# Second attention: the query and key weight chunks are multiplied by the norm's weights on POOL in place of VectorE

## The chip, the cores and the metric

The kernel runs on one core of a Trainium2 chip. The core has five engines that run side by side, each through its own list of instructions in order: TensorE (PE in the profile, its weight loads PEld), VectorE (DVE), ScalarE (ACT), GpSimd (POOL) and SyncE (SP), which here only issues DMAs. Semaphores make one engine wait for another. The metric is the device time of one execution in microseconds (us).

## The reference

The reference is an encoder trunk of two layers over 512 frames of 1024 features in float32. The first layer is latent attention with 8 heads and a SwiGLU feed-forward part of 2816 hidden features. A shared key and value is then projected from the result, and the second layer attends to it with 16 heads of 64 features and a learned bias by relative position, followed by another SwiGLU part. Every part stands between two RMS norms. What concerns the change is the input of the second attention:

```
def rms_norm(x, g):
    y = x * lax.rsqrt(jnp.mean(x * x, axis=-1, keepdims=True) + EPS)
    return y * g

h  = rms_norm(x, attn_pre_g[1]);  q  = h @ w_q
kv = rms_norm(x, g_src) @ w_kv          # keys and values
```

The norm's weight g belongs to an input feature, so it can be multiplied into the rows of w_q and w_kv in place of x.

## The kernel before

Activations lie transposed, features on the 128 partitions and the 512 frames along a row. A float32 product is made from three float32r matmuls: each operand is split into a rounded part hi (ScalarE, a cast, line 144, or a scaled copy, line 148) and the rest lo = raw - hi (VectorE, line 145 or 149), and hi·hi, lo·hi and hi·lo are added up in PSUM (mm3, lines 356 to 358). So every weight goes once through ScalarE and once through VectorE.

The class Feed brings the weights. Its plan is a list of chunks of 128x1024, in the order of use. load issues a chunk's DMA on SP into one of 5 buffers "raw", two chunks ahead of split, and split writes whi and wlo, one chunk ahead of use. A chunk of the shared values (in_w_v) has two norm weights per partition, which enter as the scale of lines 148 and 149. A chunk of queries or keys (in_w_qkb) has eight, one for every 128 columns; the list gain holds them as a broadcast 128x8x128, and VectorE multiplies the raw chunk by it in place (line 306) ahead of the split. There are 16 such chunks, two (query, key) for each of eight pairs of heads. The plan has four value chunks, the first two of these, four value chunks, and then the other fourteen.

Around the first of these chunks the feed-forward part of layer 1 ends. Its last step is the class After: the sums of squares ss go through line 1288 and 1289 (VectorE) into ssv, POOL takes the power -0.5 (line 1292, tile r), ScalarE scales the result y by it (line 1298), TensorE transposes y (line 1319, tile yt), and VectorE adds it to the residual x (line 1322), which is split into xh and xl. This is done for each half of the frames; between the transposes stand the matmuls of the values on the half that is ready. Then the squares of x are summed (acc, line 426), POOL takes the power for the norm of the second attention (line 452, r), VectorE copies it to rtk (line 1493), TensorE spreads it (line 469, bc) and ScalarE scales the values by it. In the attention TensorE is kept busy by a generator (fill_b) that makes the queries and keys of the next pair of heads between the scores of this one; POOL writes a masked corner into each head's bias tile (line 1502).

The order of instructions on each engine is set by a scheduler when the kernel is built, from the order of the code, priorities (first) and its own estimates of time.

Of the kernel before, what the change touches and what calls it, by code (L numbers as in the profile page):

```python
# [14 lines left out]
OP = mybir.AluOpType  # L15
# [53 lines left out]
def trunk(ctx: ExitStack, tc: tile.TileContext, a, out):  # L69
    nc = tc.nc  # L70
    V = nc.vector
# [10 lines left out]
    def name_(n):  # L82
        uid[0] += 1
        return f"{n}_{uid[0]}"

    def U(dt=F32, name="u"):
        return up.tile([P, S], dt, tag="u", name=name_(name), bufs=NU)
# [4 lines left out]
    def bank(tag="mm", name="b"):  # L92
        return ps.tile([P, S], F32, tag=tag, name=name_(name), bufs={"mm": 4, "s": 2, "t": 2}[tag])
# [49 lines left out]
    def split(dst_hi, dst_lo, src):  # L143
        return (nc.scalar.copy(dst_hi, src),  # L144
                V.tensor_tensor(dst_lo, src, dst_hi.bitcast(F32), op=OP.subtract))  # L145

    def split_scaled(dst_hi, dst_lo, src, col):
        return (nc.scalar.activation(dst_hi, src, AF.Copy, scale=col),  # L148
                V.scalar_tensor_tensor(dst_lo, src, col, dst_hi.bitcast(F32), op0=OP.mult, op1=OP.subtract))  # L149

    class Pair:
# [13 lines left out]
        def load(self, j):  # L165

            if j == 0:
                self.raw[4], self.raw[5] = self.tile(2), self.tile(3)
            elif j in (1, 2):
                self.raw[j] = self.tile(j - 1)  # L170
# [81 lines left out]
    class Feed:  # L252
# [20 lines left out]
        def load(self, i):  # L273
            while len(self.raw) <= min(i, len(self.plan) - 1):
                src, n, j, _ = self.plan[len(self.raw)]
                if isinstance(src, Down):
                    src.load(*j)
                    self.raw.append(None)
                    continue
                if isinstance(src, Pair):  # L280
                    src.load(j)
                    self.raw.append(None)
                    continue
                t = wp.tile([P, 1024], F32, tag="raw", name=name_("raw"), bufs=5)
                if self.gate is not None:
                    nc.gpsimd.tensor_copy(t[:1, :1], self.gate[:1, :1])
                nc.sync.dma_start(t[:, :n], src[:, :n])
                self.raw.append(t)

        def split(self, i):  # L290
            while len(self.ready) <= min(i, len(self.plan) - 1):
                j = len(self.ready)
                self.load(j + 2)
                raw, (src, n, gain, room) = self.raw[j], self.plan[j]
                for f in range(j, min(j + 8, len(self.plan))):
                    if f < j + 5 and isinstance(self.plan[f][0], Pair) or isinstance(self.plan[f][0], Down):
                        self.load(f)
                if isinstance(src, Down):
                    src.sums(*gain)
                    raw = src.at[gain]  # L300
                elif isinstance(src, Pair):
                    src.sums(gain)
                    raw = src.raw[gain]
                elif gain is not None and gain.shape[1] > 2:
                    rv = raw[:, :n].rearrange("p (a b) -> p a b", a=gain.shape[1])
                    V.tensor_tensor(rv, rv, gain, op=OP.mult)
                    gain = None
                if room is None:
                    at_ = 24 if isinstance(src, Pair) else 0
                    pieces = [tuple(wp.tile([P, 1152], F32R, tag=t, name=name_("w" + t), bufs=3)[:, at_:at_ + 1024]  # L310
                                    for t in ("hi", "lo"))]
                else:
                    pieces = self.room[room]()
                w = pieces[0][0].shape[1]
                if isinstance(raw, list):
                    c = 0
                    for t in raw:
                        c_ = slice(c, c + t.shape[1])
                        split(pieces[0][0][:, c_], pieces[0][1][:, c_], t)
                        c += t.shape[1]  # L320
                for c in range(0, 0 if isinstance(raw, list) else n, w):
                    m = min(w, n - c)
                    with ExitStack() as st:
                        for b in self.behind.get(j, ()):
                            st.enter_context(tc.issue_after(b.ins))
                        if gain is None or isinstance(src, Pair):
                            split(pieces[c // w][0][:, :m], pieces[c // w][1][:, :m], raw[:, c:c + m])
                            continue
                        for d in range(0, m, S):
                            split_scaled(pieces[c // w][0][:, d:d + S], pieces[c // w][1][:, d:d + S],  # L330
                                         raw[:, c + d:c + d + S], gain[:, (c + d) // S, 0:1])

                def at(c, m, pieces=pieces, w=w):
                    o = c % w
                    return tuple(t[:, o:o + m] for t in pieces[c // w])

                self.ready.append(at)
# [142 lines left out]
    class Head:  # L480
# [19 lines left out]
        def turn(self, qt):  # L500
            if self.pt is None:
                self.pt = [pool[0].tile([P, NQT, S], F32R, tag=t, name=name_(t), bufs=n)
                           for t, n in (("pth", 2), ("ptl", 1))]
            n = P * (qt + 1)
            p = self.p.pop(qt)
            t = bank("t", "pt")
            for kt in range(qt + 1):
                nc.tensor.transpose(t[:, kt * P:(kt + 1) * P], p[:, kt * P:(kt + 1) * P], ident)  # L508
            tv = t[:, :n].rearrange("p (a b) -> p a b", b=P)
            q_ = slice(qt * P, (qt + 1) * P)  # L510
            split(self.pt[0][:, :qt + 1, q_], self.pt[1][:, :qt + 1, q_], tv)
# [155 lines left out]
    class Split:  # L667
# [5 lines left out]
        def each(self, k, h):  # L673
            c = HALF[h]
            if len(self.xs) <= k:
                self.xs.append((U(F32R, "xh"), U(F32R, "xl")))
            t = cut(self.xs[k], c)
            if self.gain is None:
                split(*t, self.x[k][:, c])
            else:  # L680
                split_scaled(*t, self.x[k][:, c], g(self.gain, k))
# [111 lines left out]
    for j in range(2):  # L793
        t = U(name="ckv")
# [49 lines left out]
    for j in range(2):  # L844
        V.tensor_tensor(ckv[j], ckv[j], rkv, op=OP.mult)
        h, l = U(F32R, "ckh"), U(F32R, "ckl")
        feed.behind[13] = feed.behind[14] = split(h, l, ckv[j])
        cks.append((h, l))
# [740 lines left out]
    b = [bank(), bank(), bank("s"), bank("s")]  # L1589
# [101 lines left out]
```

## Time and profile before

| | |
|---|---|
| median of 3 runs | 1132.62 us (1131.86 to 1137.13) |
| profiled execution | 1131.57 us, of which the span is 1129.8 us |
| TensorE busy | 1108.2 us (98%) |
| VectorE busy | 931.9 us (82%) |
| ScalarE busy | 686.0 us (61%) |
| POOL busy | 74.9 us (7%) |
| chain that ended last | TensorE 86%, VectorE 6%, ScalarE 3% |

The span is the time from the first to the last instruction in the profiler's record; the execution's own time is a little longer. A busy share is the time in which an engine ran an instruction; matmuls overlap, so a busy TensorE need not be at its peak. The chain is followed back from the last instruction, at each step to what released it. Around the change the span reads like this: to 535 us the feed-forward part of layer 1 ends, from 527 to 590 the values and the first query and key are made, from 597 to about 740 runs the second attention.

### The profile page before, as it was taken

What the parts mean: (1) busy time and instruction counts of PE and PEld (TensorE: products, weight loads), DVE (VectorE), ACT (ScalarE), POOL (GpSimd) and SP (SyncE); (2) the same over time, 40 slices, a digit from 0 to 9 for tenths busy, and PEclk for the clock granted to TensorE, in tenths of its full rate; (3) what the DMA queues carried; (4) which work ended last, traced back from release to release, by engine and by line L of the source; (5) the groups of instructions that cost most, each with busy time, mean ns of one, the idle gap of its engine ahead of it and who ended that gap; (6) DMA issues with size and microseconds to landing.
All of it is one profiled execution on the core that took longest, in us unless ns stands there. A gap on an engine that the chain in (4) does not pass through costs nothing.

```text
span 1129.8 us, 18992 instructions
## 1 busy us (share of the span) xinstructions
PE 1108.2 (98%) x6973; PEld 984.7 (87%) x6973; DVE 931.9 (82%) x1671; ACT 686.0 (61%) x1339; POOL 74.9 (7%) x106
## 2 busy tenths in 40 slices
PE   8999999999999999999999999999999999999997
PEld 6888889899999998887788888779899999998885
DVE  7787738999899889978757977647999999889977
ACT  6476637755555566668536777546755555566685
POOL 2200000100000002401000000000100000002402
PEclk9999999999999999999999999999999999999999
DMA  7433125323322449852356656625323322449923
GB/s 235 111 109 94 57 85 196 131 87 100 109 98 94 140 149 262 140 195 61 144 149 168 154 155 158 166 88 186 131 82 106 104 102 94 139 169 281 173 59 75
DMA packets 62990, 150.85 MB, mean 134 GB/s; under 512 B 8432, under 2 KB 10224, under 8 KB 62896
## 3 DMA queue, kind: packets, MB, share of 16 engines
q1 hardware_dynamic: 55552, 136.61, 38.3%
q0 software_dynamic: 6912, 12.59, 6.8%
q8 instruction: 55, 0.90, 0.3%
q10 hardware_dynamic: 432, 0.44, 0.1%
q14 instruction: 39, 0.32, 0.1%
HBM read 119.52 MB, written 9.63 MB: 114 GB/s over the span
## 4 chain that ended last, share of the span: by engine, by line
PE 86%; DVE 6%; ACT 3%; issue 2%; DMA 1%; POOL 1%; POOLq 0%; SPq 0%; DVEq 0%; ACTq 0%
PE al L1425 17%; PE b L356 10%; PE b L357 10%; PE b L358 10%; PE be L1425 9%; PE al L1185 8%; PE ga L1425 4%; PE be L1185 4%; PE de L1185 3%; PE ga L1185 3%; PE pt L508 2%; DVE wlo L145 1%; ACT whi L144 1%; PE b L1549 1%; PE b L1550 1%
## 5 line engine op out<-in xcount | busy, mean ns | idle before, releaser
L144 ACT CAST whi<-raw 128x1024 fp32r<-128x1024 f32 (+3 forms) x224 | 225.5, 1008 | 220.5 <-PE al L1425 73.3
L145 DVE TENSOR_TENSOR wlo<-raw,whi 128x1024 fp32r<-128x1024 f32 (+3 forms) x224 | 261.1, 1167 | 62.0 <-ACT whi L144 60.3
L1425 PE MATMUL al<-th,whi 128*128 128x256 f32 x432 | 123.0, 285 | 0.1
L1425 PE MATMUL al<-th,wlo 128*128 128x256 f32 x432 | 121.3, 281 | 0.0
L1425 PE MATMUL al<-tl,whi 128*128 128x256 f32 x432 | 121.1, 280 | 0.0
L356 PE MATMUL b<-xh,whi 128*128 128x512 f32 (+1 forms) x304 | 116.4, 383 | 1.8 <-ACT xh L148 1.8
L357 PE MATMUL b<-xl,whi 128*128 128x512 f32 (+1 forms) x304 | 112.8, 371 | 0.3 <-DVE xl L149 0.3
L358 PE MATMUL b<-xh,wlo 128*128 128x512 f32 (+1 forms) x304 | 112.7, 371 | 0.0
L174 DVE TENSOR_TENSOR raw<-raw,raw 128x1024 f32<-128x1024 f32 x72 | 86.7, 1220 | 0.6 <-DMA raw<-in_w_pair 0.3
L1425 PEld LDWEIGHTS al<-th,whi 128*128 128x128 f32 x432 | 81.3, 188 | 2.4 <-DVE ut L1437 0.3
L1425 PEld LDWEIGHTS al<-th,wlo 128*128 128x128 f32 x432 | 81.3, 188 | 0.3 <-DVE wlo L145 0.3
L1425 PEld LDWEIGHTS al<-tl,whi 128*128 128x128 f32 x432 | 81.4, 188 | 0.0
L496 ACT ACTIVATE p<-p,mn 128x128 f32<-128x128 f32 (+1 forms) x96 | 54.0, 562 | 31.8 <-DVE mn L494 31.6
L145 DVE TENSOR_TENSOR ptl<-pt,pth 128x128 fp32r<-128x128 f32 (+1 forms) x96 | 46.2, 486 | 28.8 <-ACT pth L144 23.0
L144 ACT CAST whi<-wd 128x512 fp32r<-128x512 f32 x86 | 49.9, 619 | 26.8 <-PE al L1185 11.9
L145 DVE TENSOR_TENSOR wlo<-wd,whi 128x512 fp32r<-128x512 f32 x86 | 56.5, 687 | 11.5 <-ACT whi L144 11.2
L356 PEld LDWEIGHTS b<-xh,whi 128*128 128x128 f32 x304 | 57.5, 189 | 9.6 <-ACT xh L148 2.7
L358 PEld LDWEIGHTS b<-xh,wlo 128*128 128x128 f32 x304 | 57.4, 189 | 8.9
L357 PEld LDWEIGHTS b<-xl,whi 128*128 128x128 f32 x304 | 57.5, 189 | 7.3 <-DVE xl L149 0.6
L144 ACT CAST pth<-pt 128x128 fp32r<-128x128 f32 (+1 forms) x96 | 40.3, 424 | 28.4 <-PE pt L508 27.8
L1185 PE MATMUL al<-whi,ph 128*128 128x512 f32 x132 | 51.9, 393 | 0.5 <-ACT y L1238 0.5
L1185 PE MATMUL al<-whi,pl 128*128 128x512 f32 x132 | 51.5, 390 | 0.0
(308 smaller groups left out, 3274.0 us busy)
## 6 DMA issues: line engine op xcount, KB each, us to landing
raw<-in_w_pair SPq DMA_DIRECT2D x72, 512.0 KB, 3.5
wd<-in_w_down SPq DMA_DIRECT2D x54, 256.0 KB, 5.9
raw<-in_w_o SPq DMA_DIRECT2D x16, 512.0 KB, 3.6
raw<-in_w_gu SPq DMA_DIRECT2D x16, 512.0 KB, 3.7
raw<-in_w_down SPq DMA_DIRECT2D x16, 512.0 KB, 4.4
raw<-in_w_qkb SPq DMA_DIRECT2D x16, 512.0 KB, 3.6
wd<-in_w_down POOLq DMA_DIRECT2D x22, 256.0 KB, 5.5
wd<-raw POOLq DMA_DIRECT2D x22, 256.0 KB, 4.2
```

The lines of the kernel that those rows point to most:

```text
L144: return (nc.scalar.copy(dst_hi, src), V.tensor_tensor(dst_lo, src, dst_hi.bitcast(F32), op=OP.subtract))
L145: V.tensor_tensor(dst_lo, src, dst_hi.bitcast(F32), op=OP.subtract))
L174: V.tensor_tensor(t, x, y, op=OP.add)
L356: nc.tensor.matmul(o, l[0], r[0], start=start, stop=False)
L357: nc.tensor.matmul(o, l[0], r[1], start=False, stop=False)
L358: nc.tensor.matmul(o, l[1], r[0], start=False, stop=stop)
L496: nc.scalar.activation(p[:, :n], p[:, :n], AF.Exp, bias=mn[:, :1], scale=-1.0, accum_out=self.sums[:, qt:qt + 1])
L508: nc.tensor.transpose(t[:, kt * P:(kt + 1) * P], p[:, kt * P:(kt + 1) * P], ident)
L1185: nc.tensor.matmul(to[e], l[c], r[d], start=j < 4 and k == 0 and n == 0, stop=k == NF // 2 - 1 and n == 2, skip_group_check=True)
L1425: nc.tensor.matmul(o, l[c], r[d], start=first_ and n == 0, stop=k == K2 - 1 and n == 2, skip_group_check=True)
L1549: nc.tensor.matmul(o[:, q_], vv, pth[:, kt, q_], start=kt == 0, stop=False)
L1550: nc.tensor.matmul(o[:, q_], vv, ptl[:, kt, q_], start=False, stop=kt == NQT - 1)
```

## The change

The multiplication by the norm's weights moves from split, where VectorE does it, to load, where POOL does it as soon as the chunk's DMA has landed. It is the same product, in place, on the same chunks; the value chunks are left as they were.

```diff
         def load(self, i):
             while len(self.raw) <= min(i, len(self.plan) - 1):
                 src, n, j, _ = self.plan[len(self.raw)]
+                gain = j
                 if isinstance(src, Down):
...
                 nc.sync.dma_start(t[:, :n], src[:, :n])
+                if gain is not None and gain.shape[1] > 2:
+                    rv = t[:, :n].rearrange("p (a b) -> p a b", a=gain.shape[1])
+                    nc.gpsimd.tensor_tensor(rv, rv, gain, op=OP.mult)
                 self.raw.append(t)
...
                 elif gain is not None and gain.shape[1] > 2:
-                    rv = raw[:, :n].rearrange("p (a b) -> p a b", a=gain.shape[1])
-                    V.tensor_tensor(rv, rv, gain, op=OP.mult)
                     gain = None
```

The scheduler places the new instructions. On POOL, from the last DMA of the feed-forward part on, this stood before (r is the power of line 1292 or 452, bias a head's bias tile):

```order
L250 DMA wd_5334<-raw_4942 128x512
L1292 TENSOR_TENSOR r_5979<-ssv_5099,mhalf 128x2
L1502 MEMSET bias_6440 64x64
L1502 MEMSET bias_6687 64x64
L1502 MEMSET bias_6832 64x64
L1292 TENSOR_TENSOR r_6187<-ssv_5099,mhalf 128x2
L452 TENSOR_TENSOR r_6436<-v_6434,mhalf 128x4
L1502 MEMSET bias_6938 64x64
```

In the changed kernel, whose lines after the edit have numbers that are 2 higher and where line 291 is the multiplication, it is this:

```order
L250 DMA wd_5334<-raw_4942 128x512
L291 TENSOR_TENSOR raw_6225<-raw_6225,gains 128x1024
L1294 TENSOR_TENSOR r_5979<-ssv_5099,mhalf 128x2
L1504 MEMSET bias_6441 64x64
L1504 MEMSET bias_6689 64x64
L1504 MEMSET bias_6834 64x64
L291 TENSOR_TENSOR raw_6245<-raw_6245,gains 128x1024
L1294 TENSOR_TENSOR r_6187<-ssv_5099,mhalf 128x2
L291 TENSOR_TENSOR raw_6584<-raw_6584,gains 128x1024
L454 TENSOR_TENSOR r_6437<-v_6435,mhalf 128x4
L291 TENSOR_TENSOR raw_6617<-raw_6617,gains 128x1024
```

Each of the three powers now has one multiplication directly ahead of it. The other thirteen multiplications follow, eight of them ahead of the fourth bias memset and the rest between the memsets.

On VectorE, around ssv of the second half (line 1289), this stood before:

```order
L149 SCALAR_TENSOR_TENSOR wv_6246<-raw_6205,gains,wv_6246 128x512 x2
L1289 SCALAR_TENSOR_TENSOR ssv_5099<-ss_0_5097,ssv_5099 128x2
L145 TENSOR_TENSOR wlo_6311<-raw_6225,whi_6310 128x1024
L426 TENSOR_TENSOR acc_6326<-acc_6326,sq_6328 128x256
L306 TENSOR_TENSOR raw_6244<-raw_6244,gains 128x1024
L426 TENSOR_TENSOR acc_6326<-acc_6326,sq_6331 128x256
L426 TENSOR_TENSOR acc_6326<-acc_6326,sq_6334 128x256
```

And now:

```order
L149 SCALAR_TENSOR_TENSOR wv_6248<-raw_6205,gains,wv_6248 128x512 x2
L1291 SCALAR_TENSOR_TENSOR ssv_5099<-ss_0_5097,ssv_5099 128x2
L145 TENSOR_TENSOR wlo_6312<-raw_6225,whi_6311 128x1024
L428 TENSOR_TENSOR acc_6327<-acc_6327,sq_6329 128x256
L428 TENSOR_TENSOR acc_6327<-acc_6327,sq_6332 128x256
L428 TENSOR_TENSOR acc_6327<-acc_6327,sq_6335 128x256
```

The multiplication is gone from between the additions, and the rest is as it was. SP's order of the chunks' DMAs stays the same here. In the attention itself, from the scores of the first heads on, the order of TensorE, VectorE and ScalarE differs in many places by a few instructions, since the scheduler weaves the queries and keys of the next heads into a changed timing.

## Rows read from the trace of the kernel before

**Rows 1.** The page's first part: busy time and share of each engine
```profile
PE 1108.2 (98%) x6973; PEld 984.7 (87%) x6973; DVE 931.9 (82%) x1671; ACT 686.0 (61%) x1339; POOL 74.9 (7%) x106
```

**Rows 2.** Windows: PE, PEld, DVE, ACT, POOL busy, clock, DMA, GB/s; last line 306 alone
```profile
720.00:740.00 20.00, 18.85 (x97) 14.19 (x96) 14.24 (x37) 13.06 (x34) 0.00 (x0) 1.00 0.52 131
...
600.00:660.00 60.00, 59.77 (x331) 50.08 (x330) 52.00 (x122) 43.96 (x111) 0.87 (x6) 1.00 0.65 169
...
600.00:660.00 60.00, 7.28 (x6) 1.00 0.65 169
```

**Rows 3.** TensorE's waits, 530 to 660 us: in total, times, longest
```profile
PE yt L1319 <- ACT y L1298: 2.9, 1, 2.9
```

**Rows 4.** The chain that ended last, 533 to 541 us: start, us, what
```profile
537.36 1.34 ACT y L1298 x2
...
538.74 0.69 PE yt L1319 x2
```

**Rows 5.** POOL's timeline: start, us, line, operation, idle before and releaser
```profile
512.40 0.83 POOL L1292 TENSOR_TENSOR r<-ssv,mhalf 128x2 f32<-128x2 f32 x1 [34.92 <-DVE ssv L1289]
...
533.98 3.35 POOL L1292 TENSOR_TENSOR r<-ssv,mhalf 128x2 f32<-128x2 f32 x1 [20.48 <-DVE ssv L1289]
557.55 1.01 POOL L452 TENSOR_TENSOR r<-v,mhalf 128x4 f32<-128x4 f32 x1 [20.23 <-DVE v L448]
...
777.96 0.70 POOL L452 TENSOR_TENSOR r<-v,mhalf 128x2 f32<-128x2 f32 x1 [59.74 <-DVE v L448]
792.02 2.21 POOL L452 TENSOR_TENSOR r<-v,mhalf 128x2 f32<-128x2 f32 x1 [13.37 <-DVE v L448]
```

**Rows 6.** VectorE's timeline around the power at 533.98
```profile
532.35 1.41 DVE L149 SCALAR_TENSOR_TENSOR wv<-raw,gains,wv 128x512 fp32r<-128x512 f32 x2
533.67 0.16 DVE L1289 SCALAR_TENSOR_TENSOR ssv<-ss,ssv 128x2 f32<-128x2 f32 x1
533.75 1.22 DVE L145 TENSOR_TENSOR wlo<-raw,whi 128x1024 fp32r<-128x1024 f32 x1
534.88 0.42 DVE L426 TENSOR_TENSOR acc<-acc,sq 128x256 f32<-128x256 f32 x1
535.22 1.22 DVE L306 TENSOR_TENSOR raw<-raw,gains 128x1024 f32<-128x1024 f32 x1
536.35 0.42 DVE L426 TENSOR_TENSOR acc<-acc,sq 128x256 f32<-128x256 f32 x1
540.25 0.43 DVE L426 TENSOR_TENSOR acc<-acc,sq 128x256 f32<-128x256 f32 x1 [3.48 <-ACT sq L425]
```

**Rows 7.** VectorE's timeline around the power at 792.02
```profile
792.12 1.22 DVE L174 TENSOR_TENSOR raw<-raw,raw 128x1024 f32<-128x1024 f32 x1
793.26 0.42 DVE L426 TENSOR_TENSOR acc<-acc,sq 128x256 f32<-128x256 f32 x1
```

**Rows 8.** The window behind TensorE's wait, columns as in rows 2
```profile
538.50:541.50 3.00, 2.76 (x8) 2.17 (x9) 0.43 (x1) 2.95 (x8) 0.00 (x0) 0.50 0.15 60
```

**Rows 9.** Line 306 (ns min/median/max); POOL's nearest multiplication (busy us, mean ns)
```profile
L306 DVE TENSOR_TENSOR raw<-raw,gains x16: 1173/1222/1226, 500.6 to 657.1; 128x1024 f32<-128x1024 f32 x16
...
L969 POOL TENSOR_TENSOR kr<-kr,sik 64x512 f32<-64x512 f32 x1 | 1.3, 1292 | 0.1
```

**Rows 10.** The second chunk's DMA issue on SP, and its time to landing
```profile
529.11 0.33 SPq L287 DMA_DIRECT2D raw<-in_w_qkb x1
...
DMA to landing us min/median/max: 3.4/3.4/3.4
```

**Rows 11.** VectorE around the power at 557.55, and TensorE's use of rtk
```profile
555.38 1.23 DVE L306 TENSOR_TENSOR raw<-raw,gains 128x1024 f32<-128x1024 f32 x1 [1.13 <-DMA raw<-in_w_qkb]
...
559.04 0.16 DVE L1493 COPY rtk<-r 128x4 f32<-128x4 f32 x1
...
560.98 0.49 PE L469 MATMUL bc<-ident,rtk 128*128 128x128 f32 x3
```

**Rows 12.** ScalarE's timeline: the cast of the third chunk
```profile
578.69 1.05 ACT L144 CAST whi<-raw 128x1024 fp32r<-128x1024 f32 x1 [4.10 <-issue]
```

## Prediction

> **What bounds the kernel now.** I read the page's first part, the windows over the second attention, TensorE's waits there, the chain at the one long wait, and last VectorE and POOL row by row around it. TensorE is busy for 1108.2 of 1129.8 us, VectorE for 931.9, POOL for 74.9 [rows 1]. In the stretch from 600 to 660 us, where six of the sixteen multiplications run, TensorE is busy for 59.77 of 60 us and VectorE for 52.00, of which the multiplications are 7.28 [rows 2]. So VectorE is heavily loaded there, but TensorE hardly ever waits for it.
>
> TensorE has one long wait between 530 and 660 us: 2.9 us before the transposes of line 1319 [rows 3]. The chain shows what stands behind it: POOL's power r of line 1292 runs from 533.98 to 537.33 [rows 5], ScalarE scales y by it (line 1298), and TensorE transposes y at 538.74 [rows 4]. This power is a 128x2 instruction. The same form takes 0.70 us at 777.96 and 2.21 at 792.02 [rows 5]; here it takes 3.35. What differs is VectorE: in the two slow cases it runs instructions on two SBUF operands back to back. At 533.75 these are a split, an addition, the multiplication of line 306 and an addition, to 536.77, and the power ends 0.56 us later [rows 6]; at 792.12 they are a sum and an addition, to 793.69, and it ends 0.54 us later [rows 7]. VectorE's own instructions keep their length (1.22 us). I read this as POOL being held off while VectorE works through such a run.
>
> The wait also costs clock. In the 3 us behind it TensorE is granted 0.50 of its clock (the 1.2 GHz level) [rows 8], where the stretches above have 1.00 (2.4 GHz) [rows 2]. Its 2.76 us of work there, eight matmuls, would take half as long at the full level: about 1.4 us lost.
>
> **The change, part by part.** VectorE loses sixteen multiplications of 1.22 us [rows 9], 19.5 us. POOL gets them. The trace has no POOL multiplication of 128x1024; the nearest is 64x512 at 1.29 us [rows 9], and twice the elements per partition make 2.58 us, my estimate, so 41 us in all on POOL, which was busy for 0.87 us between 600 and 660 [rows 2]. The bounds are 1.2 us (VectorE's own time, if POOL's cost were mostly fixed) and 5.2 us (twice as long, since POOL's 128x2 power is stretched three- to fivefold beside a busy VectorE). I take 2.58, the row of the same kind of instruction.
>
> *Relief of VectorE in the attention.* From 600 to 660 us TensorE has 0.23 us of idle time in all [rows 2], so the 7.28 us taken off VectorE can return no more than that there. The changed order also weaves some of TensorE's heads differently. I take 0 us. The ends are -0.5 (this idle time and as much around it) and +1.2 (a badly woven stretch: from 720 to 740 us TensorE is busy for 18.85 of 20 [rows 2]).
>
> *The thirteen multiplications behind the three powers.* Their lead is read from the third chunk: it is multiplied at 555.38, when it lands [rows 11], and its cast on ScalarE comes only at 578.69 [rows 12]. A POOL instruction of 2.58 or 5.2 us is hidden in these 23 us. The memsets of the bias tiles now stand between multiplications on POOL; each serves a head that begins later, and a delay of one multiplication is hidden too. 0 us.
>
> *The first chunk.* It stands ahead of the first power r of line 1292, at 512.40. VectorE's own multiplication of it begins at 500.6 [rows 9], so the chunk has landed by then; even 5.2 us of POOL end by 505.8, 6.6 us before that power [rows 5]. If VectorE is held for 2.58 us there and saved only 1.22, it is 1.4 us late. I take 0, with ends 0 and +1.4.
>
> *The second chunk: the term that counts.* The order puts its multiplication on POOL directly ahead of the power that this chain waits for. Queued behind it are that power, then ScalarE's scaling, the transposes, and TensorE with all that follows. The chunk is issued at 529.11 and lands 3.4 us later, at 532.5 [rows 10], 1.5 us before the power was begun. VectorE is in the wv splits then, which go over into ssv and the run [rows 6]. Without line 306 the run ends earlier: from 535.22 to 536.35 is 1.13 us, so it ends at 536.77 - 1.13 = 535.64. If POOL gets through only when the run ends, the multiplication goes from 535.64 to 538.22 and the power, 0.70 us alone, ends at 538.92 in place of 537.33: +1.6 us. If the multiplication gets in ahead of the wv splits and holds VectorE, ssv itself comes some 2.5 us late, the split and the additions follow, and the power ends at about 538.9 as well. The lower end is a multiplication that runs beside VectorE from its landing, 532.5 to 535.1; the power then waits only for the shorter run, 535.64 + 0.56 = 536.2, which is -1.1. The upper end is a multiplication of 5.2 us after the run: 535.64 + 5.2 + 0.70 = 541.5, or +4.2. I take +1.6. TensorE has nothing else in its order during this wait, so it goes to the end in full. I expect the half clock to last as long as before, the 3 us after TensorE resumes.
>
> By the Trainium skill (SBUF — State Buffer, "Who interferes with whom") a VectorE instruction with two SBUF inputs and a GpSimd instruction that reads SBUF exclude each other for one whole instruction, and the later one waits for the earlier. The power came during the split, which ended at 534.97; by the rule it would have been done near 535.6, and the trace has 537.33, after three more instructions [rows 6], so the rule falls short of this row. By the rule the multiplication would get in at the end of a wv split, at 533.76, and hold VectorE to 536.3; ssv and one split would follow, and the power would end near 538.3: +0.9, and a sum of 1132.5 in place of the row's 1133.2.
>
> *The third chunk.* It stands ahead of the power of line 452, which makes rtk. It lands at 555.38 (VectorE's multiplication waited 1.13 us for it) and POOL would be done at 557.96. The power began at 557.55, so it is 0.4 us late and, at 1.01 us, ends at 558.97. Before, the copy rtk stood behind a multiplication on VectorE until 559.04 [rows 11], and that goes. TensorE asks for rtk at 560.98 [rows 11]. So 0 us; with 5.2 us it would be 560.6 + 1.0 + 0.2 = 561.8, +0.8.
>
> **The sum.** The profiled execution took 1131.57 us (span 1129.8 and 1.77 around it). With +1.6 and four terms of 0 that is 1133.2. The median of the three runs, 1132.62, lies 1.05 above the profiled one, and on that account it is 1134.2. I take 1133.5.
>
> **Rivals.**
>
> 1. *POOL gets the shorter run.* The multiplication is over before the power is due, and the power profits from the missing line 306. It ends at 536.2; transposes at 537.6; the wait is 1.8 us in place of 2.9, and if the clock then does not fall, 1.4 us more is gained: -2.5, 1129 us. For it speaks the landing at 532.5, 1.5 us ahead; against it, that VectorE is in the wv splits, on two SBUF operands, when the chunk lands, and that the power was held off by such work.
>
> 2. *POOL is slow beside VectorE.* The multiplication takes 5.2 us: +4.2 at the second chunk, +0.8 at the third: 1136.6 us. For it speak the stretched powers; against it, that VectorE has nothing to do after 535.64 until 540 [rows 6].
>
> 3. *POOL holds VectorE, and VectorE becomes the bound (slower).* If each multiplication stops VectorE for its 2.58 us, VectorE has 52.00 - 7.28 + 6 x 2.58 = 60.2 us of work in the 60 us from 600 on. It decides only from there: with less than 15.3 us of stops VectorE still has slack. Then the 6 x 1.36 us that a stop is longer than the old instruction come through: +8.2, and with the second chunk's 1.6, 1141.4 us. Against it speaks that most of VectorE's work there has one operand in PSUM, and that in no row here did a VectorE instruction grow beside POOL. The Trainium skill's rule cited above is what speaks for it; no row here has a long POOL instruction beside such VectorE work.
>
> **How the numbers follow.** Forecast 0.57 (its own range 1131.5 to 1135.5), rival 1 0.18, rival 2 0.15, rival 3 0.10. Half a per cent, 5.7 us, is about what a measurement of this kernel can tell from no change, so only times under 1127 or over 1138.3 count as a change. Rival 3 is nearly all of "slower", with the far end of rival 2: 0.10. "Faster" needs the whole wait, its clock and all idle time of the attention (2.9 + 1.4 + about 1): 0.03. The rest, 0.87, is within. The range is 1128.5 to 1138: it takes in rivals 1 and 2, and leaves out rival 3.
>
> **What would show it.** In the changed kernel's profile POOL's sixteen multiplications should take about 2.6 us each; the second should end after 538 and the power behind it near 539; TensorE's wait at line 1319 should be about 4.5 us; the half clock should again last about 3 us; TensorE should stay over 99% busy from 600 to 660 us, with VectorE near 45 of 60. A wait of under 2 us at line 1319 makes rival 1 right, a multiplication of 4 us or more rival 2, and VectorE splits of over 2 us, with TensorE under 57 of 60, rival 3.

## The result, and the profile after

The changed kernel takes 1135.81 us (median of 20 runs, 1132.59 to 1140.95), the kernel before 1132.57 (20 runs): a ratio of 1.0032, 95% interval 1.0023 to 1.0041. That is 3.2 us slower, less than the half per cent named in the prediction, but clearly not zero.

The profiled execution is one of the longer ones: 1139.7 us, 3.9 above its median. Its first part, and four stretches of it, each row with the columns of [rows 2]:

```profile
span 1137.9 us, 19029 instructions
PE 1112.2 (98%) x6973; PEld 985.9 (87%) x6973; DVE 928.5 (82%) x1655; ACT 685.7 (60%) x1339; POOL 106.6 (9%) x122
```
```profile
8.00:12.00 4.00, 4.00 (x11) 3.13 (x12) 3.21 (x6) 3.20 (x7) 1.90 (x5) 0.57 0.75 235
540.50:543.50 3.00, 3.00 (x13) 2.51 (x12) 1.39 (x4) 2.52 (x8) 0.00 (x0) 0.57 0.32 126
600.00:660.00 60.00, 57.36 (x309) 46.72 (x309) 47.29 (x109) 41.01 (x105) 11.85 (x13) 1.00 0.60 156
664.00:667.00 3.00, 3.00 (x11) 2.45 (x10) 1.68 (x6) 1.59 (x4) 0.00 (x0) 0.50 0.72 218
```

VectorE is busy for only 931.9 - 928.5 = 3.4 us less, although 19.5 us of multiplications left it: 14.5 of them are back as longer instructions, of the kind that the next rows show. From 600 to 660 us TensorE now lacks 2.64 us of 60, where it lacked 0.23 [rows 2].

To see where a kernel falls behind, I take the n-th matmul of TensorE's record in both and subtract its start. The two spans differ by 8.1 us. The changed kernel is already 1.3 us behind at 521 us. It falls behind by 1.6 from 8 to 12 us, in code that is the same and where this execution was granted 0.57 of the clock. The other ten kernels below fall behind in that place too, by 0.9 to 2.4 us, five of them at the full clock: the profiled execution of the kernel before was quick there, and that part isn't the change's. Across the second chunk's place (the matmuls at 521 and 558 us before) the lag goes from 1.29 to 1.41, through the making of the queries and keys to 591 it stays, and across the attention (591 to 732) it grows by 6.9. Behind that nothing more comes.

Around the second chunk this is POOL's timeline, columns as in [rows 5], and then VectorE's:

```profile
534.03 2.11 POOL L291 TENSOR_TENSOR raw<-raw,gains 128x1024 f32<-128x1024 f32 x1 [19.23 <-ACT sq L427]
536.90 1.54 POOL L1294 TENSOR_TENSOR r<-ssv,mhalf 128x2 f32<-128x2 f32 x1 [0.76 <-DVE ssv L1291]
556.82 1.91 POOL L291 TENSOR_TENSOR raw<-raw,gains 128x1024 f32<-128x1024 f32 x1 [18.37 <-DMA raw<-in_w_qkb]
558.83 1.01 POOL L454 TENSOR_TENSOR r<-v,mhalf 128x4 f32<-128x4 f32 x1
559.81 1.90 POOL L291 TENSOR_TENSOR raw<-raw,gains 128x1024 f32<-128x1024 f32 x1
```
```profile
532.23 1.41 DVE L149 SCALAR_TENSOR_TENSOR wv<-raw,gains,wv 128x512 fp32r<-128x512 f32 x2
533.56 0.15 DVE L1290 SCALAR_TENSOR_TENSOR ssv<-ss,eps 128x2 f32<-128x2 f32 x1
533.63 3.06 DVE L149 SCALAR_TENSOR_TENSOR wv<-raw,gains,wv 128x512 fp32r<-128x512 f32 x2
536.61 0.15 DVE L1291 SCALAR_TENSOR_TENSOR ssv<-ss,ssv 128x2 f32<-128x2 f32 x1
536.68 1.21 DVE L145 TENSOR_TENSOR wlo<-raw,whi 128x1024 fp32r<-128x1024 f32 x1
...
559.87 1.87 DVE L1495 COPY rtk<-r 128x4 f32<-128x4 f32 x1 [1.12 <-POOL r L454]
```
```profile
PE yt L1321 <- ACT y L1300: 2.8, 1, 2.8
```

POOL takes 1.90 us for a multiplication that nothing disturbs. The second one begins as its chunk lands, and one of two wv splits stretches: the pair takes 3.06 us where the pair ahead of it takes 1.41. It ends at 536.69, 0.55 us after POOL's 536.14. The power ends at 538.44, 0.55 us after the split wlo. The wait of TensorE is 2.8 us, where it was 2.9 [rows 3], and a stretch at half clock follows, as it did [rows 8].

The loss sits in the attention. TensorE's waits from 600 to 750 us, columns as in [rows 3], first two of the kernel before, whose longest there is 0.5 us, and then the changed kernel's:

```profile
PE sc L1541 <- DVE mn L494: 0.4, 1, 0.4
PE rs L1570 <- DVE ptl L145: 0.3, 1, 0.3
...
PE sc L1543 <- DVE mn L496: 2.1, 4, 0.7
PE rs L1572 <- DVE ptl L145: 1.8, 1, 1.8
PE pt L510 <- ACT pth L144: 0.5, 1, 0.5
PE pt L510 <- DVE ptl L145: 0.4, 1, 0.4
```

VectorE at 598 and 604 us and around the chunk at 615 us, and POOL there, each from its timeline:

```profile
598.44 2.40 DVE L145 TENSOR_TENSOR f<-f,fh 128x512 f32<-128x512 f32 x1
...
604.58 0.69 DVE L145 TENSOR_TENSOR f<-f,fh 128x512 f32<-128x512 f32 x1
...
615.24 2.40 DVE L145 TENSOR_TENSOR f<-f,fh 128x512 f32<-128x512 f32 x1
617.56 0.28 DVE L496 CUSTOM_DVE_ANT_0 p<-sc,bias 128x128 f32<-128x128 f32 x1
```
```profile
614.96 2.13 POOL L291 TENSOR_TENSOR raw<-raw,gains 128x1024 f32<-128x1024 f32 x1 [1.12 <-ACT fh L144]
```

And the chain that ended last, from 657 to 664 us, columns as in [rows 4]:

```profile
658.02 1.13 DVE wlo L145
659.15 2.33 DVE f L145
...
661.51 0.68 DVE of L1558
...
662.23 0.30 DVE ptl L145
...
662.58 0.66 PE rs L1572 x4
```

f of line 145 is a difference of two operands in SBUF. It takes 0.69 us at 604.58. Beside a multiplication on POOL it takes 2.40, and it ends (617.64) 0.55 us after POOL does (617.09). What I call a stop below is the time by which such an instruction is longer than the same form in the kernel before. From 600 to 690 us there are five stops, of 0.5 to 1.73 us and 6.0 us together; in the kernel before there is none. No engine waits there for a product of POOL or for a memset that stands behind one. VectorE works in its written order, so the next head's maximum (mn) and the low half of p (ptl) come late, and TensorE, whose order is written too, waits for them. The chain shows one such case whole: f is stopped, of and ptl follow, and TensorE's rs waits 1.8 us. Behind this wait the clock is at half (the window from 664 to 667 us). The trace has it at half for 3.4 us, which cost this execution a further 1.7 us or so, my estimate.

### The profile page after: what moved, and what is told of

Same layout as the page of the kernel before. It is cut to its first block, busy times and chain, and to the rows that moved or that the text cites. A ratio compares the mean times of both kernels' runs of the same rounds, so it can differ in the third digit from the quotient of the medians.

```text
span 1137.9 us, 19029 instructions
## 1 busy us (share of the span) xinstructions
PE 1112.2 (98%) x6973; PEld 985.9 (87%) x6973; DVE 928.5 (82%) x1655; ACT 685.7 (60%) x1339; POOL 106.6 (9%) x122
## 5 line engine op out<-in xcount | busy, mean ns | idle before, releaser
L245 POOL DMA_DIRECT2D wd<-in_w_down x22 | 19.6, 918 | 448.2 <-DVE raw L235 212.0
```

What stands on the lines that cost most here:

```text
L245: nc.gpsimd.dma_start(p, self.src[0, e, :, c * S:c * S + S], accum_op=OP.add)
```

## The experiments

The theory after the result: POOL's multiplication stops VectorE's instructions on two SBUF operands, and the price arises where TensorE needs VectorE at once, in the attention. The rival: the price comes from the order on POOL, with a multiplication ahead of each power.

All times are medians of runs beside the kernel before on the same chip; the lags are read from one profile of each kernel as above, in us against the profile of before: what is added across the second chunk's place (521 to 558), from there to 591, and across the attention (591 to 732).

| kernel | us (runs) | ratio to before, 95% | lag: second chunk | to 591 | attention |
|---|---|---|---|---|---|
| the change | 1135.81 (20) | 1.0032 [1.0023, 1.0041] | +0.1 | 0.0 | +6.9 |
| e1_no_mult | 1130.78 (11) | 0.9981 [0.9971, 0.9990] | -2.8 | 0.0 | -0.4 |
| e2_first_ten | 1132.18 (11) | 0.9993 [0.9984, 1.0002] | -0.2 | 0.0 | +0.1 |
| e9_last_six | 1136.79 (6) | 1.0047 [1.0033, 1.0061] | +0.3 | 0.0 | +5.0 |
| e3_both | 1143.24 (4) | 1.0097 [1.0083, 1.0111] | -0.2 | +1.7 | +9.3 |
| e5_pieces | 1134.20 (11) | 1.0012 [1.0001, 1.0023] | +0.8 | 0.0 | +0.6 |
| e4_scalar | 1138.37 (5) | 1.0052 [1.0039, 1.0065] | +4.1 | +1.1 | +0.4 |
| e6_one_input | 1132.53 (11) | 0.9999 [0.9989, 1.0009] | +0.2 | 0.0 | -0.1 |
| e7_power_first | 1129.37 (6) | 0.9970 [0.9959, 0.9982] | -3.1 | 0.0 | 0.0 |
| e8_ten_behind | 1129.22 (6) | 0.9972 [0.9960, 0.9983] | -2.8 | 0.0 | 0.0 |
| e10_all_behind | 1133.10 (12) | 1.0016 [1.0006, 1.0025] | -2.8 | 0.0 | +3.4 |

In every row but the first, whose profile is a long execution, the three lags together are within 1.3 us of the measured difference.

**No multiplication.** e1_no_mult leaves the multiplication by the norm's weights out on both engines; its matmuls stand in the changed kernel's order.

```diff
-                if gain is not None and gain.shape[1] > 2:
-                    rv = t[:, :n].rearrange("p (a b) -> p a b", a=gain.shape[1])
-                    nc.gpsimd.tensor_tensor(rv, rv, gain, op=OP.mult)
```

> The changed kernel with the sixteen multiplications left out on both engines (the norm's weights are missing from queries and keys). TensorE, VectorE and ScalarE have word for word the order of the changed kernel. Stops theory (POOL's multiplications hold up VectorE's instructions on two SBUF operands in the attention, and TensorE waits for those): the loss goes, 1130 to 1132 us, TensorE's waits from 600 to 680 us under 1 us. Order theory (the attention's new weave of instructions costs by itself): the time stays at 1135 to 1136 us with about the same waits. Powers theory (the three powers behind POOL's multiplications cost): the loss goes too, but the time is got back before 600 us.

It took 1130.78 us, 5 less than the changed kernel, and 1.9 less than before. So the matmuls' new order isn't what costs, and the sixteen instructions on POOL are. Without line 306 and without POOL's multiplication the wait for y is 1.4 us, and no half clock follows:

```profile
PE yt L1318 <- ACT y L1297: 1.4, 1, 1.4
...
530.00:545.00 15.00, 13.55 (x67) 10.56 (x66) 11.91 (x27) 12.11 (x34) 1.88 (x1) 1.00 0.70 236
```

**The first ten, or the last six.** The last six chunks are those that land in the attention. Their multiplications alone go back to VectorE, and in the other kernel they alone stay on POOL.

```diff
-                if gain is not None and gain.shape[1] > 2:
+                if gain is not None and gain.shape[1] > 2 and on_pool(src):
...
+    def on_pool(src):
+        pr = (src.offset - a["w_qkb"].offset) // (2 * P * 1024)
+        return pr < 5
```

(pr counts pairs of chunks; e9_last_six has pr >= 5.)

> POOL multiplies the first ten chunks, which are multiplied before the attention is under way; VectorE multiplies the last six as before. TensorE has word for word the order of the kernel before. Stops theory and order theory: 1132 to 1133.5 us, as before. Powers theory: all its cost is here, so 1135 us or more.

> The last six chunks (those cast between 600 and 660 us) are multiplied on POOL when they land, the first ten on VectorE as before: the counterpart of the kernel with the first ten on POOL, which took 1132.2 us. Theory of the stops: the whole price of the change lies in the attention, so 1135 to 1137 us, some 3 us or more over the kernel before, with VectorE's instructions stretched to over 2 us at about five places between 600 and 690 us, none elsewhere, and the long wait before the transposes of y as before. Rival, that the price lies in the order around the powers: as before, 1132 to 1133 us.

The first: 1132.18 us, no difference from before. Three of its ten multiplications stand ahead of the powers, and five stops are there (7.8 us together, all before 600 us), so neither the order nor stops as such cost anything. The second: 1136.79 us, the whole price. The row is its window in the attention, behind it stand its five stopped instructions there, and last the multiplication on POOL beside the third:

```profile
600.00:680.00 80.00, 76.31 (x410) 61.74 (x409) 61.59 (x140) 51.26 (x128) 13.33 (x13) 1.00 0.60 154
...
606.31 2.40 DVE L145 TENSOR_TENSOR f<-f,fh 128x512 f32<-128x512 f32 x1
618.31 2.39 DVE L145 TENSOR_TENSOR f<-f,fh 128x512 f32<-128x512 f32 x1
626.84 1.76 DVE L145 TENSOR_TENSOR wlo<-raw,whi 128x1024 fp32r<-128x1024 f32 x1 [0.61 <-ACT whi L144]
632.62 2.02 DVE L145 TENSOR_TENSOR f<-f,fh 128x512 f32<-128x512 f32 x1
647.76 1.65 DVE L145 TENSOR_TENSOR ol<-of,oh 128x512 fp32r<-128x512 f32 x1 [0.69 <-ACT oh L144]
...
625.62 1.90 POOL L296 TENSOR_TENSOR raw<-raw,gains 128x1024 f32<-128x1024 f32 x1 [5.38 <-ACT pth L144]
```

The stops are 6.2 us together (three of them make an instruction longer than 2 us, where about five were expected). TensorE's lag grows by 5.0 us beside them, although VectorE is busy for only 61.6 of 80 us and the clock stays full: by 1.6 beside the first, 1.3 beside the second, 1.4 beside the third and fourth, and 0.7 behind. The rival falls.

**Stops on the old load.** e3_both keeps POOL's multiplications and gives VectorE its old number back, by ones.

```diff
+                    rv = raw[:, :n].rearrange("p (a b) -> p a b", a=gain.shape[1])
+                    V.tensor_tensor(rv, rv, ones.unsqueeze(2).to_broadcast([P, KT, P]), op=OP.mult)
```

> POOL multiplies all sixteen chunks when they have landed, and VectorE multiplies each once more, by ones, where the kernel before multiplied it. The weave of the attention is nearly that of the kernel before, and VectorE is not relieved. Stops theory: POOL's stops come on top of the old load, 1136 to 1140 us, with VectorE splits of over 1.5 us in the trace. Order theory: as before, 1132 to 1133.5 us.

1143.24 us, 10.6 over before and above the range that was expected. Most of this isn't the stops: from 600 us on there are only two, 1.8 us together. VectorE's multiplication by ones has to wait for POOL's product of the same chunk, six times and 8.8 us in all from 591 us on, two of them here:

```profile
605.38 1.22 DVE L310 TENSOR_TENSOR raw<-raw,ones 128x1024 f32<-128x1024 f32 x1 [3.11 <-POOL raw L291]
...
639.77 1.23 DVE L310 TENSOR_TENSOR raw<-raw,ones 128x1024 f32<-128x1024 f32 x1 [1.72 <-POOL raw L291]
```

Neither the kernel before nor the changed one has such waits. So this run tells nothing of what the relief of VectorE is worth beside the stops.

**Shorter or other instructions on POOL.** e5_pieces cuts the product in four; e4_scalar uses eight tensor_scalar of 128x128, each with one weight per partition as its factor. e6_one_input is a single tensor_scalar over the chunk; it applies the first of the eight weight columns to all of it, so seven of eight are not applied.

```diff
+                    for c in range(0, gain.shape[1], 2):
+                        nc.gpsimd.tensor_tensor(rv[:, c:c + 2], rv[:, c:c + 2], gain[:, c:c + 2], op=OP.mult)
...
+                    for c in range(gain.shape[1]):
+                        tc_ = t[:, c * P:c * P + P]
+                        nc.gpsimd.tensor_scalar(tc_, tc_, gain[:, c, 0:1], None, op0=OP.mult)
...
+                    nc.gpsimd.tensor_scalar(t[:, :n], t[:, :n], gain[:, 0, 0:1], None, op0=OP.mult)
```

> As the changed kernel, but POOL multiplies each chunk in four instructions on two tensors of 128x256 in place of one of 128x1024. TensorE, VectorE and ScalarE have the order of the changed kernel. If a stop of VectorE lasts as long as one POOL instruction (stops theory), stops shrink from 1.7 to some 0.6 us and the time is 1132 to 1134 us; POOL's work on a chunk grows to about 2.5 us. If VectorE is stopped for POOL's whole work on a chunk, 1136 to 1138 us.

> POOL multiplies each chunk in eight pieces of 128x128, each by one weight per partition (a tensor_scalar with one SBUF tensor as input) in place of one multiplication of two tensors. TensorE, VectorE and ScalarE have word for word the order of the changed kernel. Stops theory: a stop lasts at most one piece, some 0.3 us, so most of the loss goes: 1131 to 1133 us. Order theory: 1135 to 1136 us.

> As the changed kernel, but POOL multiplies each whole chunk, 128x1024, by one weight per partition: one instruction with one SBUF tensor as input (seven of the eight weights are not applied). The order is that of the changed kernel. If any long POOL instruction that reads SBUF stops VectorE, its splits are again 1.5 us and more longer and the time is 1134 to 1137 us. If only one with two tensor inputs does, VectorE's instructions keep their length beside it and the time is 1130 to 1133 us, apart from what the second chunk costs ahead of the power.

POOL's group in the changed kernel and in these three (busy us, mean ns), and under it a row or two at the second chunk: the wv splits of e5_pieces, TensorE's wait in e4_scalar, and POOL's instruction and VectorE beside it in e6_one_input:

```profile
L291 POOL TENSOR_TENSOR raw<-raw,gains 128x1024 f32<-128x1024 f32 x16 | 33.2, 2077 | 104.1 <-DMA raw<-in_w_qkb 77.7 <-ACT sq L427 19.2 <-ACT p L498 4.5
```
```profile
L292 POOL TENSOR_TENSOR raw<-raw,gains 128x256 f32<-128x256 f32 x64 | 48.3, 785 | 95.2 <-DMA raw<-in_w_qkb 71.6 <-ACT sq L428 19.2 <-ACT pth L144 3.2
...
534.37 1.77 DVE L149 SCALAR_TENSOR_TENSOR wv<-raw,gains,wv 128x512 fp32r<-128x512 f32 x2
```
```profile
L292 POOL TENSOR_SCALAR raw<-raw,gains 128x128 f32<-128x128 f32 x128 | 89.9, 722 | 75.1 <-DMA raw<-in_w_qkb 52.2 <-ACT sq L428 19.3 <-ACT fh L144 1.1
...
PE yt L1322 <- ACT y L1301: 5.6, 1, 5.6
```
```profile
L290 POOL TENSOR_SCALAR raw<-raw,gains 128x1024 f32<-128x1024 f32 x16 | 50.4, 3153 | 92.1 <-DMA raw<-in_w_qkb 63.9 <-ACT sq L426 19.2 <-ACT pth L144 4.6
...
534.11 3.64 POOL L290 TENSOR_SCALAR raw<-raw,gains 128x1024 f32<-128x1024 f32 x1 [19.24 <-ACT sq L426]
...
535.03 0.99 DVE L1290 SCALAR_TENSOR_TENSOR ssv<-ss,ssv 128x2 f32<-128x2 f32 x1
535.95 1.21 DVE L145 TENSOR_TENSOR wlo<-raw,whi 128x1024 fp32r<-128x1024 f32 x1
```

With quarters the splits take 1.77 us in place of 1.41, and no stop in the whole kernel is over 0.43 us: a stop grows with the instruction on POOL that causes it (0.61 us undisturbed here, 1.90 in the change), and stays below it. The attention's price falls to 0.6, and POOL's longer work (3.0 us a chunk, where 2.5 was expected) costs 0.8 ahead of the power; the time comes out just above the range that was expected. e6_one_input needs more of POOL than the change, 50.4 us, and costs nothing: its stops are five in all, 0.84 us at most (ssv at 535.03), and a split runs beside POOL at its usual length (535.95). So in the attention it isn't POOL's time that costs; it is the stop. e4_scalar missed its expectation: VectorE is hardly stopped (one case of over 0.13 us, the small copy rtk by 0.43), as foreseen, but eight pieces are 5.8 us a chunk, and ahead of the power TensorE's wait grew to 5.6 us. There the mechanism of the prediction's second-chunk term is seen at work, by another instruction.

**The power first.** e7_power_first is the kernel before, with the second chunk's multiplication on VectorE held behind the power (through a factor 1.0 that POOL sets after it). e8_ten_behind is e2_first_ten, and e10_all_behind the changed kernel, with POOL's multiplications from the second chunk on issued behind the powers.

```diff
+                    if src.offset == a["w_qkb"][0, 1].offset:
+                        one = consts.tile([P, 1], F32, name="one")
+                        with first(400):
+                            with tc.issue_after(power[0].ins):
+                                nc.gpsimd.memset(one, 1.0)
+                            V.scalar_tensor_tensor(rv, rv, one, gain, op0=OP.mult, op1=OP.mult)
...
+                    with ExitStack() as st:
+                        if src.offset != a["w_qkb"][0, 0].offset:
+                            st.enter_context(tc.issue_after(power[0].ins))
+                        nc.gpsimd.tensor_tensor(rv, rv, gain, op=OP.mult)
```

> The kernel before, with one change: VectorE's multiplication of the second chunk waits for a memset that POOL does right behind the power of line 1292 (it takes a factor of one from there). TensorE's order is that of the kernel before. If the power was held up in the kernel before by VectorE's run of instructions on two SBUF operands, it now ends near 535.6 in place of 537.3, TensorE's wait at line 1319 falls from 2.9 to about 1.3 us, its clock does not fall there, and the time is 1129.5 to 1130.5 us. If the power is slow for another reason, the wait is at least 2.5 us and the time 1132.6.

> POOL multiplies the first ten chunks, as in the second experiment, but from the second chunk on behind the power of line 1292 or 452 that stood behind it; VectorE multiplies the last six. TensorE's order is that of the kernel before. Stops theory with the powers first: the wait at line 1319 is about 1.4 us as without any multiplication, no fall of the clock, 1129 to 1130.5 us. If the multiplication behind the power makes the second chunk's split late, TensorE waits for its cast near 561 us and the time is 1131 to 1133.

> All sixteen chunks are multiplied on POOL, but from the second chunk on behind the powers. Theory of the stops: the 3 us that the powers' order gave in the kernel with ten on POOL remain, and the price of the last six comes on top, so 1132 to 1134 us: about the kernel before, 2 to 3 us under the changed kernel, and 3 to 5 over the kernel with ten on POOL behind the powers (1129.2). Rival, that the order around the powers is all: 1129 us.

The power and TensorE's wait in e7_power_first, and POOL's two instructions and the wait in e8_ten_behind:

```profile
535.95 1.55 POOL L1301 TENSOR_TENSOR r<-ssv,mhalf 128x2 f32<-128x2 f32 x1 [20.48 <-DVE ssv L1298]
...
PE yt L1328 <- ACT y L1307: 1.1, 1, 1.1
```
```profile
534.70 1.88 POOL L1307 TENSOR_TENSOR r<-ssv,mhalf 128x2 f32<-128x2 f32 x1 [20.48 <-DVE ssv L1304]
536.55 1.90 POOL L301 TENSOR_TENSOR raw<-raw,gains 128x1024 f32<-128x1024 f32 x1
...
PE yt L1334 <- ACT y L1313: 1.4, 1, 1.4
```

The power takes 1.55 and 1.88 us where it took 3.35 [rows 5], since VectorE's run behind ssv no longer holds line 306. The wait falls from 2.9 to 1.1 and 1.4 us, the clock stays at its full level behind it (1.00 from 530 to 545 us), and both kernels are 3 us faster than before: the two fastest of this study, which the measurement doesn't tell apart. e10_all_behind has the same gain at the power and loses it in the attention: 1133.10 us. Put together by ratios, the last six cost 0.4 to 0.5% in each of three comparisons: e9_last_six to before (1.0047), the change to e2_first_ten (1.0032 / 0.9993 = 1.0039) and e10_all_behind to e8_ten_behind (1.0016 / 0.9972 = 1.0044). That is 4.4 to 5.3 us; the interval of the first alone is 3.7 to 6.9.

## Why the prediction came out as it did

The time lies in the range and within the half per cent, on the side that the sum gave. But the sum's one term hardly exists, and the cost stands where the sum had a zero, so that the time came out near is luck.

- **A multiplication of 2.58 us**: mis-sized. Undisturbed it is 1.90, and 33.2 us for all sixteen in place of 41.
- **"Relief of VectorE in the attention. I take 0 us"** is the step that failed. The relief alone, with the new order, is worth what was said: -0.4 in e1_no_mult, inside the end of -0.5. What the step left out is what POOL then does to the instructions that stay. I had that as rival 3, and let it decide only when VectorE runs out of slack, at 15.3 us of stops in 60. It decides from the first stop that stands ahead of something TensorE is about to need: 6.2 us of stops in e9_last_six, with VectorE busy for 61.6 of 80 us, gave 5.0. Slack as a mean over 60 us didn't hide delays of 1.7 us in a chain from TensorE through VectorE and back. That most of VectorE's work there has one operand in PSUM didn't help: f, ol and wlo have two in SBUF, and these were stopped. That no VectorE instruction grew beside POOL in the kernel before told little, since POOL had only powers and memsets there.
- **The second chunk, +1.6**: +0.1 measured (and -0.2 and +0.2 in e2_first_ten and e6_one_input). The landing, the place in the order and the wv splits held up for POOL were right, and the course of events is that of the branch with +0.9: the multiplication gets in first, VectorE's wv split, ssv and one more split follow, and then the power. Two sizes weren't. ssv came 1.65 us late relative to the rest (536.61, less the 1.29 of lag, against 533.67 [rows 6]), not 2.5. And I let the split and the additions behind ssv hold the power to 538.9; they held it to 0.55 us after the split. From ssv's start to the power's end it is now 538.44 - 536.61 = 1.83 us, where before, with line 306 in the run, it was 537.33 - 533.67 = 3.66. So 1.65 lost and 1.83 gained: both halves of the forecast and of rival 1 happened, and cancel. The half clock behind the wait came as predicted.
- **The thirteen later ones and the first, 0**: right as to their products, for which nothing waits (the first holds up a split of VectorE by 1.71 us, and no lag comes of it). The third chunk: rtk was stopped too (559.87, 1.87 us) and ended at 561.74, 0.7 us before TensorE used it at 562.4. The lag didn't move there. In e3_both and e4_scalar this lead was used up (+1.7, +1.1).
- **Rival 1**, a shorter run for the power, is what one gets when the power stands first (e7, e8: the wait falls to 1.1 and 1.4 us, -3). **Rival 2** is out: 1.90 us, not 5.2. **Rival 3** is the mechanism, at 4.4 to 5.3 us in place of 8.2, and not by load.
- Of what was to show it: VectorE's splits of over 2 us came (2.40), and TensorE's 57.36 of 60 lies between the forecast's 99% and rival 3's 57. The forecast's other signs failed: the second multiplication ended at 536.14 and not after 538, and the wait was 2.8 us and not 4.5.

A stopped instruction of VectorE starts after POOL's, and runs most of its own time once POOL's has ended: those of 128x512 (0.69 to 0.75 us alone) end 0.55 us after it, those of 128x1024 (1.21 alone) 1.08 us after it, as wlo of e9_last_six at 626.84 does. None was stopped for longer than one POOL instruction. By the Trainium skill (SBUF — State Buffer, "Who interferes with whom") a VectorE instruction with two SBUF inputs and a GpSimd instruction that reads SBUF exclude each other for a whole instruction; here the trace agrees. The one-input tensor_scalar of e6_one_input also reads SBUF, and beside it (534.11 to 537.75) VectorE's wlo ran in its usual 1.21 us (535.95 to 537.16); there the rule falls short.

What stays open: what a given stop costs. In the changed kernel the stop of f at 598.44 added nothing to the lag, and the equally long one at 615.24 added 1.3 us. The same six multiplications gave lags of 6.9, 5.0 and 3.4 us in three profiles, as the chunks landed at other moments of the heads' work; about 1.7 of the 6.9 is half clock.

## What to carry to other kernels

A product of two tensors that moves to POOL can be paid for by VectorE wherever VectorE has two operands in SBUF: count the instructions that may be stopped, and ask for each what TensorE takes from behind it in the next few microseconds; mean slack was no cover here. Move such work only into stretches where TensorE runs on results made long before (the first ten chunks cost nothing), or cut it short (no stop here was longer than one POOL instruction). A form with one tensor as input can be the better one although POOL takes longer over it: the sixteen of e6_one_input cost nothing. And keep POOL's small instruction that a chain waits for ahead of the bulk work, with a short run on VectorE behind its input: that alone gave 3 us here.

## What the runs showed of the hardware

- On POOL one tensor as input isn't faster than two: tensor_scalar over 128x1024 took 2.85 us undisturbed (mean 3.15, e6_one_input), tensor_tensor 1.90; eight tensor_scalar of 128x128 took 5.8 in the mean (e4_scalar).
- A COPY of 128x4 on VectorE, with one SBUF operand, was stopped too: 1.87 us beside POOL's multiplication at 559.81, 0.16 before [rows 11]. It ended 0.03 us after POOL's instruction. In e4_scalar a tensor_scalar of 128x128 on POOL stopped it as well (0.59 us).
- TensorE's waits of 1.1 and 1.4 us before yt (e7_power_first, e1_no_mult and e8_ten_behind) were followed by full clock (2.4 GHz), those of 1.8 and 2.8 us in the changed kernel by 3.4 us at half (1.2 GHz).
